# A decoder block on one core: activation sums of the second half step made in the out projection, and products reordered

## The chip, the cores and the metric

The kernel runs on one core of one Trainium2 chip. The metric is the device time of one execution in microseconds. Engines: TensorE (PE), which multiplies; VectorE (DVE) and ScalarE (ACT), which do the elementwise work; GpSimd (POOL); and SyncE (SP), which here issues most transfers. Each engine works through its own list of instructions in a fixed order and waits where an operand isn't ready.

## The reference, cut to what matters

```python
D_MODEL, SEQ, D_FF = 1024, 512, 2816
def rms_norm(x, gain):
    return x * lax.rsqrt(jnp.mean(x * x, axis=-1, keepdims=True) + eps) * gain
def swiglu(h, w_gate, w_up, w_down):
    return (jax.nn.silu(h @ w_gate) * (h @ w_up)) @ w_down

x = x + 0.5 * swiglu(rms_norm(x, ffn1_norm), ffn1_w_gate, ffn1_w_up, ffn1_w_down)
h = rms_norm(x, mix_norm)
g_a, g_b, z_uv, z_q, z_k, z_v = split(h @ w_in)
y_a = gmlp_chunk_mixer(z_uv, ...)                  # 8 groups, chunks of 128 positions
y_b = diff_attention(q, k, v, positions, ...)      # 8 heads, causal
m = sigmoid(g_a) * (y_a @ a_w_proj) + sigmoid(g_b) * (y_b @ b_w_proj)
x = x + m @ w_out
x = x + 0.5 * swiglu(rms_norm(x, ffn2_norm), ffn2_w_gate, ffn2_w_up, ffn2_w_down)
```

## The kernel before, in words

Everything is float32 and lies feature-major: the eight tiles `x_0` to `x_7` have 128 features by 512 positions. A product is made exactly enough by splitting each operand into a rounded part and the rest (`split`: a cast on ACT, line 139, and a subtraction on DVE, line 140) and multiplying hi by hi, hi by lo and lo by hi: three matmuls (`mm3`, lines 125 to 127). So each weight tile of 128 by 1024 costs a transfer, a cast and a subtraction before PE can use it.

The program has three parts. **Half step one** (`ffn` with pool `ff1`) and **half step two** (`ff2`) are the same function: 22 blocks of hidden features, two to a `q`, so 11 steps q = 0 to 10. The mixing stage stands between.

A step q makes gate and up products of two hidden blocks. The first two steps of either half step are plain (`plain_quad`): 4 x 24 matmuls of 512 columns. The others (`quad`) use a seven-product scheme on 2 x 2 blocks: seven products of 24 matmuls with 256 columns each. The factors are sums of weight blocks (`total`, line 311, on DVE: `w_sum`) and sums of activations (`half_sums`: `s_hi`, `s_lo`, four sums for each pair of feature tiles kt and kt + 4, lines 222 to 227, and a split). Products named A take plain activations (`xg_hi`, `xg_lo`), those named S take sums. The sums are made while the plain steps run, called at q = 1. `kept` (line 331) copies a bank out; line 350 adds S0's running result to p7 before S3 adds into the same bank. Lines 346 and 352 form the parts of g, line 357 multiplies by `r_bc`, the norm's factor for each position, line 358 is the Silu. After steps 3, 7 and 10 a group of down projections follows: eight output tiles, 24 matmuls of 512 columns each (18 in the last group), which add up in `y`. Behind the last group `y` is scaled by r (line 396) and the residual, read again into `back`, is added (line 397).

The norm's factor comes from squares on ACT (lines 186 and 189), added on DVE (190), summed over features by two matmuls with ones (195, 196), and `r_bc` on ACT and DVE (`norm_scale`). In half step one the squares are called (`prepare1`) after the first pair's products f = 0 of step 0.

In the mixing stage units of projections are pumped between the steps of attention. `turn_weights` transposes the attention weights of a head and splits them into `at_hi`, `at_lo`. The last units are `add_out`: its `evacuate` adds the out projection to `x1` (line 879), makes `xg_hi` (ACT, line 181) and `xg_lo` (DVE, line 182) for half step two, and adds squares. They run in the order n = 0, 4, 1, 5, 2, 6, 3, 7.

Tiles come from pools with a fixed number of buffers; a scheduler orders each engine's instructions from the program and the pools.

Of the kernel before, what the change touches and what calls it, by code (L numbers as in the profile page):

```python
# [58 lines left out]
def decoder_block(  # L59
# [87 lines left out]
    nc.gpsimd.dma_start(out=gains, in_=cols)  # L147
# [62 lines left out]
    def half_sums(pool, norm):  # L210
# [3 lines left out]
        def add(kt, x1, x2):  # L214
# [5 lines left out]
            f = pool.tile([P, 4, HT], F32, name="sums", tag=("a_hi", "a_lo")[kt % 2] + str(2 + kt // 2))  # L220
# [24 lines left out]
    def ffn(pool, gu, dn, norm, xt, finish, load, prepare, again):  # L245
        a_hi, a_lo = {}, {}
        add_sums, operand = half_sums(pool, norm)
# [25 lines left out]
        def plain_quad(q):  # L273
# [3 lines left out]
            for f in range(2):  # L277
# [86 lines left out]
        y, back = [], []  # L364
        for f0 in range(0, NF, 8):
            n = min(8, NF - f0)
            for q in range(f0 // 2, (f0 + n) // 2):
# [7 lines left out]
            if f0 + n == NF:  # L375
                for i in range(HK):
                    tag = ("w_sum", "g")[i // 2]
                    back.append(pool.tile([P, 2, T], F32, name="x_again", tag=tag, bufs=2))
# [667 lines left out]
```

## Time and profile before

| | |
|---|---|
| median of 3 timed runs | 1159.12 us (1158.76 to 1159.71) |
| the profiled execution | 1159.7 us, of which span 1158.0 |
| granted TensorE clock, mean | 0.997 |
| PE / PEld busy | 1146.5 (99%) / 996.1 (86%) us |
| DVE / ACT busy | 836.4 (72%) / 590.0 (51%) us |
| chain that ended last | PE 95%, ACT 2%, DVE 1%, DMA 1% |

A row of a timeline gives the start, the duration, engine, line, operation, output and inputs with shapes; in brackets stands the idle time before it on its engine and what ended it. Matmuls are pipelined, so their pace is read from start to start. `x4` after a row means four in sequence, with the time of all.

### The profile page before, as it was taken

The page shows a single profiled execution, that of the slowest core. Times are in us where ns is not written, and L with a number is a line of the kernel's source. Part 1 is how long each engine was busy: PE and PEld are TensorE (multiplying, and loading weights), DVE is VectorE, ACT ScalarE, POOL GpSimd, SP SyncE. Part 2 cuts the span into 40 slices and gives each one's busy share as a digit, 9 for nine tenths or more (in the row PEclk, how much of TensorE's full clock was granted, in tenths as well). Part 3 has the DMA queues.
Part 4 walks back from the last instruction along what each step waited for, and adds up shares of the span by engine and source line. Part 5 has one row for each costly group of instructions (what it writes and reads, how often), then busy time and mean ns, then how long its engine had stood idle before and what let it go on. Part 6 is the DMA issues. An engine that isn't in the chain of part 4 may idle for free.

```text
span 1158.0 us, 16621 instructions
## 1 busy us (share of the span) xinstructions
PE 1146.5 (99%) x6554; PEld 996.1 (86%) x6554; DVE 836.4 (72%) x1356; ACT 590.0 (51%) x856; POOL 30.5 (3%) x58
## 2 busy tenths in 40 slices
PE   8999999999999999999999999999999999999998
PEld 6898899989987888888888887888899899988996
DVE  6995389747877667877878986655887369855975
ACT  6563256424544554657587966334545235523440
POOL 0000000000003000000000000000000000000000
PEclk9999999999999999999999999999999999999999
DMA  8134232512434323222212224235424223431241
GB/s 270 58 117 138 73 97 92 163 56 82 143 131 145 122 80 91 74 91 74 74 55 66 63 76 162 91 120 164 153 74 145 73 74 110 132 122 56 83 155 72
DMA packets 46032, 122.08 MB, mean 105 GB/s; under 512 B 4355, under 2 KB 5411, under 8 KB 45955
## 3 DMA queue, kind: packets, MB, share of 16 engines
q1 hardware_dynamic: 43488, 113.26, 30.9%
q0 software_dynamic: 2464, 7.77, 1.9%
q8 instruction: 51, 0.84, 0.3%
q14 instruction: 29, 0.21, 0.1%
HBM read 114.72 MB, written 6.29 MB: 105 GB/s over the span
## 4 chain that ended last, share of the span: by engine, by line
PE 95%; ACT 2%; DVE 1%; DMA 1%; issue 0%; SPq 0%; DVEq 0%; ACTq 0%
PE bank_acc L324 20%; PE bank_att L324 11%; PE bank_acc L127 11%; PE bank_acc L125 11%; PE bank_acc L126 11%; PE bank_att L127 5%; PE bank_att L126 5%; PE bank_att L125 5%; PE bank_acc L536 4%; PE bank_acc L538 4%; PE bank_acc L537 4%; DMA x<-in_x 1%; PE bank_att L666 1%; PE bank_att L667 1%; PE bank_att L694 1%
## 5 line engine op out<-in xcount | busy, mean ns | idle before, releaser
L139 ACT CAST w_hi<-w_raw 128x1024 fp32r<-128x1024 f32 (+2 forms) x192 | 191.8, 1003 | 282.1 <-PE bank_acc L126 92.6
L140 DVE TENSOR_TENSOR w_lo<-w_raw,w_hi 128x1024 fp32r<-128x1024 f32 (+2 forms) x192 | 223.5, 1168 | 75.2 <-ACT w_hi L139 70.3
L139 ACT CAST w_hi<-w_sum 128x1024 fp32r<-128x1024 f32 x72 | 75.4, 1050 | 140.2 <-PE bank_acc L324 63.0
L324 PE MATMUL bank_acc<-s_lo,w_hi 128*128 128x256 f32 x432 | 121.6, 281 | 0.0
L324 PE MATMUL bank_acc<-s_hi,w_hi 128*128 128x256 f32 x432 | 121.5, 281 | 0.0
L324 PE MATMUL bank_acc<-s_hi,w_lo 128*128 128x256 f32 x432 | 121.4, 281 | 0.0
L140 DVE TENSOR_TENSOR w_lo<-w_sum,w_hi 128x1024 fp32r<-128x1024 f32 x72 | 87.7, 1221 | 27.6 <-ACT w_hi L139 27.6
L125 PE MATMUL bank_acc<-xg_hi,w_hi 128*128 128x512 f32 x224 | 89.5, 400 | 3.1 <-ACT w_hi L139 3.0
L127 PE MATMUL bank_acc<-xg_hi,w_lo 128*128 128x512 f32 x224 | 89.7, 400 | 1.2 <-DVE w_lo L140 1.2
L126 PE MATMUL bank_acc<-xg_lo,w_hi 128*128 128x512 f32 x224 | 89.1, 398 | 0.1
L536 PE MATMUL bank_acc<-w_hi,xg_hi 128*128 128x512 f32 x224 | 88.9, 397 | 0.0
L537 PE MATMUL bank_acc<-w_lo,xg_hi 128*128 128x512 f32 x224 | 88.6, 395 | 0.0
L538 PE MATMUL bank_acc<-w_hi,xg_lo 128*128 128x512 f32 x224 | 88.5, 395 | 0.0
L324 PEld LDWEIGHTS bank_acc<-s_hi,w_lo 128*128 128x128 f32 x432 | 81.7, 189 | 0.0
L324 PEld LDWEIGHTS bank_acc<-s_hi,w_hi 128*128 128x128 f32 x432 | 81.7, 189 | 0.0
L324 PEld LDWEIGHTS bank_acc<-s_lo,w_hi 128*128 128x128 f32 x432 | 81.6, 189 | 0.0
L125 PE MATMUL bank_att<-a_hi,w_hi 128*128 128x512 f32 x176 | 69.4, 395 | 0.0
L125 PE MATMUL bank_acc<-a_hi,w_hi 128*128 128x512 f32 x176 | 69.4, 395 | 0.0
L126 PE MATMUL bank_acc<-a_lo,w_hi 128*128 128x512 f32 x176 | 69.4, 394 | 0.0
L126 PE MATMUL bank_att<-a_lo,w_hi 128*128 128x512 f32 x176 | 69.4, 394 | 0.0
L127 PE MATMUL bank_acc<-a_hi,w_lo 128*128 128x512 f32 x176 | 69.4, 394 | 0.0
L127 PE MATMUL bank_att<-a_hi,w_lo 128*128 128x512 f32 x176 | 69.4, 394 | 0.0
(268 smaller groups left out, 2835.2 us busy)
## 6 DMA issues: line engine op xcount, KB each, us to landing
w_raw<-in_gu SPq DMA_DIRECT2D x86, 512.0 KB, 3.7
w_raw<-in_dn SPq DMA_DIRECT2D x32, 512.0 KB, 3.6
w_raw<-in_w_qk SPq DMA_DIRECT2D x16, 512.0 KB, 3.6
w_raw<-in_dn SPq DMA_DIRECT2D x16, 384.0 KB, 3.3
w_raw<-in_w_v SPq DMA_DIRECT2D x8, 512.0 KB, 3.6
w_raw<-in_w_ga SPq DMA_DIRECT2D x8, 512.0 KB, 3.5
w_raw<-in_w_gb SPq DMA_DIRECT2D x8, 512.0 KB, 3.5
w_raw<-in_w_pb SPq DMA_DIRECT2D x8, 512.0 KB, 3.5
```

What stands on the lines that cost most here:

```text
L125: nc.tensor.matmul(ps, lhsT=lhi, rhs=rhi, start=first, stop=False)
L126: nc.tensor.matmul(ps, lhsT=lhi, rhs=rlo, start=False, stop=False)
L127: nc.tensor.matmul(ps, lhsT=llo, rhs=rhi, start=False, stop=last)
L139: latest["hi"] = nc.scalar.copy(hi, src)
L140: latest["lo"] = nc.vector.tensor_tensor(lo, src, hi, op=ALU.subtract)
L324: nc.tensor.matmul(o, lhsT=l[:, s], rhs=r, start=first and f == kt == i == 0, stop=kt == HK - 1 and i == 2, skip_group_check=True,)
L536: nc.tensor.matmul(banks[t], lhsT=xg_hi[k][:, ts], rhs=hi[:, s], start=k == 0, stop=False)
L537: nc.tensor.matmul(banks[t], lhsT=xg_hi[k][:, ts], rhs=lo[:, s], start=False, stop=False)
L538: nc.tensor.matmul(banks[t], lhsT=xg_lo[k][:, ts], rhs=hi[:, s], start=False, stop=k == KD - 1)
L666: nc.tensor.matmul(s[m], lhsT=qd[m][:, qs], rhs=kd[m][:, :w], start=True, stop=False)
L667: nc.tensor.matmul(s[m], lhsT=ql[m][:, qs], rhs=kd[m][:, :w], start=False, stop=True)
L694: nc.tensor.transpose(ps[:, j * P : (j + 1) * P], a[:, j * P : (j + 1) * P], ident)
```

## The change

1. The sums of half step two (`sums2`) are made in `add_out`, for each n of 4 to 7, as the tile pair becomes complete; `s_hi` and `s_lo` lie in a pool `pairs` that lasts through the kernel, and raw weights, the halves of `at_hi` and `at_lo`, and the sums before their split in a pool `wide`.
2. Half step two has no plain steps: `plain` is 2 in half step one and 0 in half step two, so its steps 0 and 1 are quads.
3. In a quad the product A12 comes second instead of sixth, and its part of g right after it.
4. In half step one the squares and `norm_scale` are called after the splits of the second pair's weights (f = 1, k = 0).
5. The residual is read again and added in the middle group of down projections; the last group scales and adds only.
6. `at_hi` and `at_lo` are two tiles of half the size each, so that a transposed tile with over two blocks is split in two pieces. `PIECES` goes from 43 to 27, since several pieces lie in `pairs`.
7. The transfer of `gains` is issued by ACT instead of POOL; WARM goes from 8 to 6.

```diff
-    nc.gpsimd.dma_start(out=gains, in_=cols)
+    nc.scalar.dma_start(out=gains, in_=cols)
...
-            f = pool.tile([P, 4, HT], F32, name="sums", tag=("a_hi", "a_lo")[kt % 2] + str(2 + kt // 2))
+            f = room(kt)
...
-            s_hi.append(pool.tile([P, 4, HT], F32R, name=f"s_hi{kt}"))
-            s_lo.append(pool.tile([P, 4, HT], F32R, name=f"s_lo{kt}"))
+            for s, n in ((s_hi, "hi"), (s_lo, "lo")):
+                s.append(pair(f"s_{n}{kt}").rearrange("p a (b t) -> p (a b) t", t=HT))
...
+                    if q == 0 and f == 1 and k == 0:
+                        prepare[0][0](); prepare[0][1]()
...
-                if q == f == 0:
-                    prepare[0]()
...
-            for i, t in enumerate((b11, b12, b22, b21)):
+            for i, t in ((0, b11), (3, b21), (1, b12), (2, b22)):
...
             product(a, b11, "A11", True)
             p1 = kept(a)
+            product(e, b21, "A12", True)
+            nc.vector.tensor_tensor(
+                g[:, :, :HT], e.rearrange("p (f t) -> p f t", **two), p1.rearrange("p (f t) -> p f t", **two), op=ALU.add
+            )
             t3 = total(b12, b22)
             product(c, t3, "S1", True)
...
             product(a, total(b11, b12), "S0")
             nc.vector.tensor_tensor(p7, a, p7, op=ALU.add)
-            product(e, b21, "A12", True)
...
-                if q < 2:
+                if q < plain:
                     plain_quad(q)
...
-                if q == 1:
+                if q == plain - 1:
                     for kt in range(HK):
                         add_sums(kt, xt[kt], xt[kt + HK])
...
+                elif f0 + n < NF:
+                    nc.vector.tensor_tensor(y[j], y[j], ps, op=ALU.add)
+                    nc.vector.scalar_tensor_tensor(y[j], y[j], -0.5, r_bc, op0=ALU.mult, op1=ALU.mult)
+                    xr = scratch()
+                    again(xr, j)
+                    nc.vector.tensor_tensor(y[j], y[j], xr, op=ALU.add)
                 else:
...
+                    t = scratch()
+                    nc.vector.scalar_tensor_tensor(t, ps, -0.5, r_bc, op0=ALU.mult, op1=ALU.mult)
+                    nc.vector.tensor_tensor(y[j], y[j], t, op=ALU.add)
                     finish(j, y[j])
...
-            split(at_hi[:, : i + 1, qs], at_lo[:, : i + 1, qs], src)
+            src = ps.rearrange("p (j q) -> p j q", q=P)
+            for b in range(i // 2 + 1):
+                n = min(2, i + 1 - 2 * b)
+                split(at_hi[b][:, :n, qs], at_lo[b][:, :n, qs], src[:, 2 * b : 2 * b + n, :])
...
                 add_squares(n, xr)
+                if n >= HK:
+                    sums2[0](n - HK, x1[n - HK], xr)
```

Three places in the engines' lists. First DVE in the head: `w_lo` with 256 columns are the first pair's weights, with 1024 those of the pairs behind it. Before:

```order
15 L182 SCALAR_TENSOR_TENSOR xg_lo_117<-x_7_157,gains,xg_hi_109 128x512
16 L190 TENSOR_TENSOR sq_sum<-sq_sum,scratch 128x512 x6
17 L140 TENSOR_TENSOR w_lo<-w_raw,w_hi 128x1024
18 L190 TENSOR_TENSOR sq_sum<-sq_sum,scratch 128x512
19 L140 TENSOR_TENSOR w_lo<-w_raw,w_hi 128x1024 x2
20 L140 TENSOR_TENSOR sq_lo<-sq_sum,sq_hi 128x512
```

And after:

```order
15 L191 SCALAR_TENSOR_TENSOR xg_lo_121<-x_7_161,gains,xg_hi_113 128x512
16 L149 TENSOR_TENSOR w_lo<-w_raw,w_hi 128x1024 x2
17 L199 TENSOR_TENSOR sq_sum<-sq_sum,scratch 128x512 x6
18 L149 TENSOR_TENSOR w_lo<-w_raw,w_hi 128x1024
19 L199 TENSOR_TENSOR sq_sum<-sq_sum,scratch 128x512
20 L149 TENSOR_TENSOR w_lo<-w_raw,w_hi 128x1024
21 L149 TENSOR_TENSOR sq_lo<-sq_sum,sq_hi 128x512
```

Two of the weight subtractions moved ahead of the six additions of squares, and on ACT likewise two casts ahead of the squares.

Second DVE at the entry of half step two, from the last out projection's evacuation (x_7) on. Before:

```order
1019 L879 TENSOR_TENSOR x_7_7040<-x_7_7040,bank_acc 128x512
1020 L182 SCALAR_TENSOR_TENSOR xg_lo_117<-x_7_7040,gains,xg_hi_109 128x512
1021 L190 TENSOR_TENSOR sq_sum<-sq_sum,scratch 128x512
1022 L140 TENSOR_TENSOR sq_lo<-sq_sum,sq_hi 128x512
1023 L140 TENSOR_TENSOR w_lo<-w_raw,w_hi 128x1024 x4
1024 L159 SCALAR_TENSOR_TENSOR scratch<-r_bc 128x512
```

And after, where `w_sum` are the sums of weight blocks for S1 (row 1064) and S2 (row 1065):

```order
1055 L905 TENSOR_TENSOR x_7_7098<-x_7_7098,bank_acc 128x512
1056 L191 SCALAR_TENSOR_TENSOR xg_lo_121<-x_7_7098,gains,xg_hi_113 128x512
1057 L199 TENSOR_TENSOR sq_sum<-sq_sum,scratch 128x512
1058 L233 SCALAR_TENSOR_TENSOR sums<-x_3_7090,gains,scratch 128x256
1059 L234 SCALAR_TENSOR_TENSOR sums<-x_7_7098,gains,scratch 128x256
1060 L235 SCALAR_TENSOR_TENSOR sums<-x_7_7098,neg_gains,sums 128x256
1061 L236 SCALAR_TENSOR_TENSOR sums<-x_7_7098,neg_gains,sums 128x256
1062 L149 TENSOR_TENSOR s_lo_7732<-sums,s_hi_7731 128x1024
1063 L349 TENSOR_TENSOR g<-bank_att,scratch 128x2x256
1064 L320 TENSOR_TENSOR w_sum<-w_raw 128x1024
1065 L320 TENSOR_TENSOR w_sum<-w_sum,w_raw 128x1024
1066 L149 TENSOR_TENSOR w_lo<-w_sum,w_hi 128x1024 x2
```

The four sums, `s_lo`, the part of g with A12 (L349) and two sums of weights now stand between x_7 and the next `w_lo`.

Third DVE at the end of a quad of half step one, around p7 += S0 (L350 before, L363 after) and the first use of S3 (L360, L369). Before:

```order
86 L350 TENSOR_TENSOR scratch<-bank_acc,scratch 128x512
87 L140 TENSOR_TENSOR w_lo<-w_raw,w_hi 128x1024
88 L352 TENSOR_TENSOR g<-bank_att,scratch 128x2x256
89 L357 TENSOR_TENSOR g<-g,r_bc 128x1024
90 L140 TENSOR_TENSOR w_lo<-w_raw,w_hi 128x1024
91 L360 TENSOR_TENSOR g<-bank_acc,g 128x2x256
```

And after:

```order
107 L359 TENSOR_TENSOR g<-bank_att,scratch 128x2x256
108 L366 TENSOR_TENSOR g<-g,r_bc 128x1024
109 L149 TENSOR_TENSOR w_lo<-w_raw,w_hi 128x1024
110 L363 TENSOR_TENSOR scratch<-bank_acc,scratch 128x512
111 L370 TENSOR_TENSOR g<-scratch,g 128x2x256
112 L149 TENSOR_TENSOR w_lo<-w_sum,w_hi 128x1024
113 L320 TENSOR_TENSOR w_sum<-w_sum,w_raw 128x1024
114 L369 TENSOR_TENSOR g<-bank_acc,g 128x2x256
```

The multiplication by r and the weights' `w_lo` moved ahead of p7 += S0; on PE, A12's 24 matmuls no longer stand between S0 and S3, but the first matmuls of what comes next.

## Rows read from the trace of the kernel before

**Rows 1.** The page: busy time, share of the span and instructions of each engine.

```profile
PE 1146.5 (99%) x6554; PEld 996.1 (86%) x6554; DVE 836.4 (72%) x1356; ACT 590.0 (51%) x856; POOL 30.5 (3%) x58
```

**Rows 2.** Stretches: window and length, busy us (count) by engine, clock, DMA share, GB/s.

```profile
core 0: us, PE busy (x) PEld busy (x) DVE busy (x) ACT busy (x) POOL busy (x), PEclk, DMA share, GB/s
21.60:24.90 3.30, 2.90 (x7) 2.35 (x8) 3.30 (x5) 1.78 (x3) 0.00 (x0) 0.50 0.53 153
...
805.70:850.74 45.04, 45.04 (x195) 36.43 (x194) 33.89 (x46) 22.64 (x28) 0.54 (x1) 1.00 0.37 123
850.74:890.57 39.83, 39.83 (x338) 39.82 (x336) 33.96 (x34) 22.05 (x26) 0.00 (x0) 1.00 0.41 133
...
404.00:700.00 296.00, 295.23 (x1422) 241.16 (x1421) 230.63 (x610) 205.71 (x388) 10.49 (x20) 1.00 0.26 80
...
640.00:660.00 20.00, 19.85 (x103) 16.07 (x102) 17.50 (x40) 19.70 (x37) 0.00 (x0) 1.00 0.08 27
```

**Rows 3.** Timeline of PE in the head: start, us, instruction, idle before and releaser.

```profile
18.15 0.40 PE L127 MATMUL bank_att<-xg_hi,w_lo 128*128 128x512 f32 x1
20.07 0.50 PE L125 MATMUL bank_acc<-xg_hi,w_hi 128*128 128x512 f32 x1 [1.52 <-ACT w_hi L139]
...
22.00 0.80 PE L127 MATMUL bank_acc<-xg_hi,w_lo 128*128 128x512 f32 x1 [1.20 <-DVE w_lo L140]
22.59 0.63 PE L125 MATMUL bank_acc<-xg_hi,w_hi 128*128 128x512 f32 x1
...
25.07 0.39 PE L125 MATMUL bank_acc<-xg_hi,w_hi 128*128 128x512 f32 x1
```

**Rows 4.** Timeline of ACT in the head.

```profile
15.35 3.74 ACT L189 ACTIVATE scratch<-x 128x512 f32<-128x512 f32 x7
```

**Rows 5.** Timeline of DVE in the head.

```profile
16.14 4.66 DVE L190 TENSOR_TENSOR sq_sum<-sq_sum,scratch 128x512 f32<-128x512 f32 x6
20.72 1.22 DVE L140 TENSOR_TENSOR w_lo<-w_raw,w_hi 128x1024 fp32r<-128x1024 f32 x1
```

**Rows 6.** Transfers of the head: SP's queue, DMA issues at 10.1 (us to landing), ACT.

```profile
10.11 0.33 SPq L290 DMA_DIRECT2D w_raw<-in_gu  x1
...
w_raw<-in_gu SPq DMA_DIRECT2D x1, 512.0 KB, 6.2
...
5.19 0.72 ACT L181 ACTIVATE xg_hi<-x,gains 128x512 fp32r<-128x512 f32 x1 [2.88 <-DMA gains<-in_cols]
...
7.39 1.36 ACT L181 ACTIVATE xg_hi<-x,gains 128x512 fp32r<-128x512 f32 x2 [0.88 <-DMA x<-in_x]
```

**Rows 7.** Timelines of DVE and ACT, last out projection and the sums.

```profile
805.90 0.69 DVE L879 TENSOR_TENSOR x<-x,bank_acc 128x512 f32<-128x512 f32 x1 [2.22 <-PE bank_acc L127]
...
808.04 0.68 DVE L190 TENSOR_TENSOR sq_sum<-sq_sum,scratch 128x512 f32<-128x512 f32 x1
...
825.16 0.48 DVE L225 SCALAR_TENSOR_TENSOR sums<-x,gains,scratch 128x256 f32<-128x256 f32 x1
825.56 0.48 DVE L226 SCALAR_TENSOR_TENSOR sums<-x,neg_gains,sums 128x256 f32<-128x256 f32 x1
...
825.03 1.04 ACT L139 CAST s_hi<-sums 128x1024 fp32r<-128x1024 f32 x1
```

**Rows 8.** Timeline of DVE, end of a quad of half step two.

```profile
885.09 0.69 DVE L350 TENSOR_TENSOR scratch<-bank_acc,scratch 128x512 f32<-128x512 f32 x1 [0.68 <-PE bank_acc L324]
...
888.65 1.23 DVE L357 TENSOR_TENSOR g<-g,r_bc 128x1024 f32<-128x1024 f32 x1
889.80 1.22 DVE L140 TENSOR_TENSOR w_lo<-w_raw,w_hi 128x1024 fp32r<-128x1024 f32 x1
```

**Rows 9.** Attention weights, 404 to 700: count, duration ns min/median/max, forms.

```profile
L139 ACT CAST at_hi<-bank_att x32: 248/437/588, 468.7 to 690.4; 128x128 fp32r<-128x128 f32 x8, 128x256 fp32r<-128x256 f32 x8, 128x384 fp32r<-128x384 f32 x8, 128x512 fp32r<-128x512 f32 x8
L140 DVE TENSOR_TENSOR at_lo<-bank_att,at_hi x32: 281/487/692, 469.6 to 691.4; 128x128 fp32r<-128x128 f32 x8, 128x256 fp32r<-128x256 f32 x8, 128x384 fp32r<-128x384 f32 x8, 128x512 fp32r<-128x512 f32 x8
```

**Rows 10.** Timeline of DVE at the end.

```profile
1153.52 0.69 DVE L396 TENSOR_TENSOR y<-y,r_bc 128x512 f32<-128x512 f32 x1
1154.25 0.69 DVE L397 SCALAR_TENSOR_TENSOR y<-y,x_again 128x512 f32<-128x512 f32 x1
```

More of the change, by code (lines that the diff above doesn't have):

```diff
@@ L42 @@
 PI32 = 3.1415925
-PIECES = 43
+PIECES = 27
 RAWS = 2
-WARM = 8
+WARM = 6
 HK = KD // 2
@@ L103, in any_bank, with pair, wide_tile @@
         return bank(acc if turn_of[0] else att)
+    def pair(name, dtype=F32R):
+        return pairs.tile([P, 2, T], dtype, name=name, tag="pair")
+    def wide_tile(name, shape, dtype):
+        return wide.tile(shape, dtype, name=name, tag="wide")
     def scratch():
@@ L204, in norm_scale, with half_sums @@
         rsqrt_newton(r_bc, v, t)
-    def half_sums(pool, norm):
+    def half_sums(norm, room):
         s_hi, s_lo = [], []
@@ L243, in half_sums, with ffn @@
         return add, operand
-    def ffn(pool, gu, dn, norm, xt, finish, load, prepare, again):
+    def ffn(pool, gu, dn, sums, xt, finish, load, prepare, again, plain):
         a_hi, a_lo = {}, {}
-        add_sums, operand = half_sums(pool, norm)
+        add_sums, operand = sums
         turns = {"w": 0, "raw": 0}
@@ L362, in quad @@
             split(*activated(q), g)
-        y, back = [], []
+        y = []
         for f0 in range(0, NF, 8):
@@ L371, in ffn @@
                     quad(q)
-                if q == 1:
+                if q == plain - 1:
                     for kt in range(HK):
                         add_sums(kt, xt[kt], xt[kt + HK])
[L375 to L378, printed above, removed]
-                    again(back[i], i)
             for j in range(KD):
@@ L475, in prepare1 @@
                 add_squares(j, xt[j], latest["hi"])
-            norm_scale()
         def constants1():
@@ L485, in finish1, with again1, room1 @@
             nc.gpsimd.dma_start(out=x1_dram[j], in_=y)
-        def again1(t, i):
-            nc.sync.dma_start(out=t, in_=x[:, 2 * i : 2 * i + 2, :])
-        ffn(ff1, gu1, dn1, 0, xt, finish1, load1, {0: prepare1, 5: constants1}, again1)
+        def again1(t, j):
+            nc.sync.dma_start(out=t, in_=x[:, j, :])
+        def room1(kt):
+            return ff1.tile([P, 4, HT], F32, name="sums", tag=("a_hi", "a_lo")[kt % 2] + str(2 + kt // 2))
+        ffn(ff1, gu1, dn1, half_sums(0, room1), xt, finish1, load1, {0: (prepare1, norm_scale), 5: constants1}, again1, 2)
     x1 = []
@@ L495, in decoder_block @@
         half = mix.enter_context(tc.tile_pool(name="half", bufs=PIECES))
-        big = mix.enter_context(tc.tile_pool(name="big", bufs=1))
-        mask = big.tile([P, T], F32, name="mask")
+        only = mix.enter_context(tc.tile_pool(name="only", bufs=1))
+        mask = only.tile([P, T], F32, name="mask")
         nc.gpsimd.memset(mask, 0.0)
@@ L566, in evacuate @@
             def evacuate(t, ps):
-                take = lent if b else piece
-                hi, lo = take(f"v_hi{b}_{t}"), take(f"v_lo{b}_{t}")
+                if b:
+                    hi, lo = lent(f"v_hi{t}"), lent(f"v_lo{t}")
+                else:
+                    v = pair(f"v{t}")
+                    hi, lo = v[:, 0], v[:, 1]
                 r = r_tok[:, t : t + 1]
@@ L688, in turn_weights @@
             if i == 0:
-                weights[h] = [big.tile([P, NT, T], F32R, name=f"at_{n}", tag=f"at_{n}") for n in ("hi", "lo")]
+                weights[h] = [
+                    [wide_tile(f"at_{n}{b}", [P, 2, T], F32R) for b in range(2)] for n in ("hi", "lo")
+                ]
             at_hi, at_lo = weights[h]
@@ L833, in evacuate @@
             def evacuate(ps):
-                store[n] = piece(f"{name}{n}", F32)
+                if name == "ga" and n < 4:
+                    store[n] = piece(f"{name}{n}", F32)
+                elif n % 2 == 0:
+                    t = pair(f"{name}{n}", F32)
+                    store[n], store[n + 1] = t[:, 0], t[:, 1]
                 nc.vector.tensor_tensor(store[n], ps, r_bc, op=ALU.mult)
@@ L958, in finish2, with again2 @@
             nc.sync.dma_start(out=out[:, j, :], in_=y)
-        def again2(t, i):
-            for e in range(2):
-                nc.sync.dma_start(out=t[:, e], in_=x2_dram[2 * i + e])
-        ffn(ff2, gu2, dn2, 2, x1, finish2, None, {0: norm_scale}, again2)
+        def again2(t, j):
+            nc.sync.dma_start(out=t, in_=x2_dram[j])
+        ffn(ff2, gu2, dn2, sums2, None, finish2, None, {0: norm_scale}, again2, 0)
 def _layouts(i):
```

27 lines of the change are left out of this document (12 added, 15 removed).

## The prediction

> **What bounds the kernel now.** I read the page's engine table first. TensorE (PE) is busy 1146.5 of 1158.0 us, 99%; VectorE (DVE) 72%, ScalarE (ACT) 51% [rows 1]. So time falls only if PE gets fewer columns, or if the few microseconds in which it does not run at its pace go. Second, the busy time by stretch shows what that pace is: two plain steps take 45.04 us, with two matmuls of the norm 194 of 512 columns, so 0.232 us each; two quads take 39.83, and in them the weight loads (PEld) are as busy as PE itself [rows 2]. Third, I looked for places where PE starts late. From the first plain step on there is one: the head. At 18.15 the last matmul of the first pair starts; the next should at 18.38 and does at 20.07 (waiting for `w_hi`), two later comes 22.00 (waiting for `w_lo`), and then six run some 0.42 us apart until 25.07 [rows 3]; the granted clock there is 0.50, that is 1.2 GHz for 2.4 [rows 2]. Ten starts from 18.15 to 25.07 should be 2.32 us and are 6.92: 4.60 lost. The cause is on ACT and DVE: seven squares stand on ACT from 15.35 to 19.09 ahead of the casts of the next weights [rows 4], and six additions of squares on DVE from 16.14 to 20.80 ahead of the first `w_lo` [rows 5]. The mixing stage loses little: PE is busy 295.23 of 296, but ACT runs at 19.70 of 20 in its densest part [rows 2].
>
> All sums below are made against the profiled execution, 1159.7 us; the three timed runs have their median 0.58 lower (1159.12), so I take 0.6 off at the end. A measurement of this kernel can tell about 0.2%, 2.3 us, from no change.
>
> **1. The squares of the first step move behind the weights.** The raw tile that PE wants at 18.38 lands at 10.11 + 6.2 = 16.31 [rows 6]. ACT is free by then (its squares start at 15.35 [rows 4]), so the cast (1.04 for this shape [rows 7]) runs 16.31 to 17.35, the `w_lo` (1.22 [rows 5]) to 18.6, and the first gap closes. The second raw tile, issued right behind, I take as landed 1.2 later (nothing on the page gives it alone; PE wants it only after 24 matmuls more, but what follows on ACT moves with it): cast to 18.6, `w_lo` to 19.9. Then come eight squares of 3.74/7 = 0.53 [rows 4], ACT until 22.9, six additions of 4.66/6 = 0.78 [rows 5], DVE until 24.5. The next pair's first `w_hi` comes at 23.9 but its `w_lo`, behind the additions, at 25.8; PE's order after the change takes 24 matmuls and two more before it, 18.38 + 26 x 0.232 = 24.4. A stall of 1.4 stays where 4.60 were: **-3.2** (-2.0 if the clock falls in it too, -4.6 if there is none). WARM 6 and the earlier `gains` give nothing: the first k waits for `gains` at 5.19, but the second waits for x at 7.39 anyway [rows 6].
>
> **2. Two plain steps of the second half step become quads.** 45.04 - 39.83, less two matmuls of the norm (2 x 0.23), which are in the plain stretch and stay in any case [rows 2]: **-4.75**. It holds as far as a quad keeps its pace of 39.83/336 = 0.1185 us per matmul of 256 columns.
>
> The rows show PEld busy 39.82 of 39.83 in quads and 36.43 of 45.04 in the plain steps [rows 2]. The Trainium skill, "TensorE: Matmul & The Clock Gate", section "LDWEIGHTS (loading the stationary operand)", takes a weight load as its 128 columns over 1.2, some 107 ns; by it a quad of 168 matmuls, bound by its loads, is an estimated 17.9 us, term 2 about -8.7 and the result about 1155.8. The trace disagrees, with 118.5 ns per matmul over 336 of them, and the measurement decides: I give that rule no chance here.
>
> **3. A new wait at the entry of the second half step.** Before, the first plain steps need only `xg`, and the sums are made beside them. After, the first quad's third product (S1) needs `s_lo` of the last pair of feature tiles, whose x7 comes out of the last out projection. Walked with the durations of before: DVE adds x7 at 805.90, and the `sq_sum` behind it ends 808.72; four sums 0.40 apart end 810.43; cast of the sums 1.04, to 811.5; `s_lo` 1.22, to 812.77 [rows 7]. Here the order of DVE decides (the excerpt): behind `s_lo` stands g = A12 + p1 (L349, 0.69), and only behind that the sum of weights for S1 (1.22, to 814.5), its cast on ACT (to 815.6), the sum for S2 on DVE (to 815.8), then `w_lo` (to 816.9) [rows 5, 7, 8]. PE has A11 from 805.70 to 808.54 and A12 to 811.39, and would start S1's third matmul at 811.63; it starts at 816.97. **+5.3**, between 4.2 (if `s_lo` comes earlier, L349 still waits for the end of A12) and 5.6 (if every hand-over costs 0.05 more). In the other 19 quads the weights of S1 stand ahead of L349 in DVE's order, so this happens once. In the out projection the other three sets of sums (4 x 0.40 + 1.22, 2.8 us each two units) lie in DVE's idle time, 2.22 us a unit [rows 7].
>
> The head shows what such a wait costs beyond itself: after PE idled to 20.07 and to 22.00 the granted clock fell from 2.4 to 1.2 GHz [rows 2], and six matmuls took 2.48 instead of 1.39 us [rows 3]; with the one at 22.00 (0.59 to the next instead of 0.23) that is 1.45. PE idles longer here. **+1.45**, between 0 and 2.3.
>
> **4. The order of products in a quad.** Before, S0 is followed by A12's 24 matmuls, 2.84 us, then S3, which adds into the bank that p7 += S0 (L363, L350 before) has to have read. After, A12 is gone from there; in PE's order 9 to 17 matmuls of the next A11 (1.07 to 2.0 us), or five of the down projection (1.16; four, 0.93, before the last groups), stand between. In before's quad p7 += S0 starts at 885.09 with DVE idle ahead of it [rows 8]; after, g x r (1.22) and `w_lo` (1.15 apart) come first. Walked quad by quad through DVE's order, L363 ends 1.05 us after S0 in most, 1.3 to 1.45 where a weight sum more is ahead. Against 0.93 to 1.16 that is 0 to 0.04 in nine quads, 0.3 to 0.45 in some five: **+1.5** (0.3 to 3.5). What hides it is DVE's spare time: 33.9 of 39.8 busy over two quads [rows 2].
>
> **5. The mixing stage.** The attention weights lie in halves, so for i = 2 and 3 of each head there is one more cast and one more subtraction: 16 each. From 248 ns for 128 columns to 588 for 512 a cast is 0.135 fixed, a subtraction (281 to 692) 0.14 [rows 9], 2.2 and 2.3 us in all. But in the changed kernel the second half's cast waits for the first half's subtraction on DVE, about 0.42, and ACT stands: some 0.5 to 0.7 each, 8 to 11 us of ACT spread over 220 us in which ACT has 70% [rows 2]. PE is ahead of ACT in most of it. **+1.0** (-1 to +4; below zero since the order of some other rows there shifts too, by one row in ten).
>
> **6. The tail.** After the last matmul three dependent operations run on DVE, 0.73 apart [rows 10]; the change leaves two: **-0.7**. The residual is read earlier, in the middle down group, where a unit is 24 matmuls (5.56) and DVE has about 1.9 more: nothing.
>
> Sum: -3.2 - 4.75 + 5.3 + 1.45 + 1.5 + 1.0 - 0.7 = +0.6, so 1160.3 in a profiled execution and **1159.7** for the median. What the plain steps give, the wait at their place takes back.
>
> **Rivals.** *Faster: only what is certain.* S3 finds its bank read in time, the split halves stay beside PE's work, and the clock holds through the stall: -3.2 - 4.75 + 5.3 - 0.7 = -3.35, 1155.8. For it: DVE has 15% free in quads, ACT 30% in the mixing stage; against it: the stall is longer than the one that halved the clock in the head.
> *Slower: ACT in the mixing stage.* The second cast of each half waits on DVE while queries, keys and scores of the next step queue behind it on ACT. If half of the 11 us reaches PE, term 5 is 5.5 instead of 1.0: +5.1, 1164.2. It decides the sign from about 2 us more than term 5 on. For it: ACT at 19.70 of 20 [rows 2] where PE already shows 0.15 us idle; against it: that is one part of the stage only.
> *The new wait isn't there*, because the weights of S1 come early enough: without term 3 the sum is -6.15, 1153.0. Only if DVE's order on the chip were another than listed, or the last sums much faster.
>
> **How the numbers follow.** Forecast 0.44, faster rival 0.25, slower rival 0.24, no wait 0.07. Within the forecast's own range, 1157 to 1162, most is within 2.3 us of 1159.12: same 0.36, faster 0.03, slower 0.05. The faster rival gives 0.20 faster, 0.05 same; the slower 0.22 and 0.02; the last 0.07 faster. Together faster 0.30, same 0.43, slower 0.27. The range 1155.0 to 1164.5 holds both rivals' middles and leaves out the last and the slower one's upper end. Signs on both sides hold most of the chance, so the forecast's own range, 1157 to 1162, stands beside it.
>
> **What will show it.** The head: PE without the gap at 18.4, one of about 1.4 near 24.4, no half clock. The entry of the second step: PE idle some 4 us at A12's end and 1.1 before S1's third matmul, released by `w_hi` and `w_lo` of the weight sum, with half clock behind it. Quads: gaps of 0 to 0.45 before the first S3, released by DVE L363. Mixing: PE busy within 1 us of 295.2. Two additions in the tail. I am wrong if the entry's stall is under 4 or over 6, if PE idles over 3 us more in the mixing stage, or if quads of 19.92 grow by more than 0.2 each.

## The result and the profile after

| | before | after |
|---|---|---|
| median of the timed runs | 1158.94 us (1158.12 to 1159.71, 4 runs) | 1167.65 us (1165.87 to 1169.58, 4 runs) |
| ratio | | 1.008 (1.0067 to 1.0092) |
| the profiled execution, its span | 1159.7, 1158.0 us | 1167.16, 1165.5 us |

The change makes the kernel slower by 0.8%, some 9 us. The forecast was no change, 1159.7 in 1155.0 to 1164.5.

The engine table of the changed kernel's page, to set beside [rows 1]:

```profile
PE 1147.3 (98%) x6694; PEld 999.0 (86%) x6694; DVE 866.3 (74%) x1406; ACT 605.1 (52%) x887; POOL 28.6 (2%) x57
```

PE's busy time hardly moved although two plain steps became quads: a PE that runs slowly, or that starts 0.1 us late, counts as busy. DVE has 30 us more, ACT 15. So the stretches have to be compared. The boundaries in both traces are the same instructions: the start, the first matmul of step 4 of half step one, the first of the attention part of the mixing stage, of the out projections, of step 4 of half step two, and the end. The columns are window, length, busy time by engine, clock, DMA share, GB/s. The kernel before:

```profile
0.00:141.14 141.14, 135.62 (x739) 116.62 (x739) 96.06 (x117) 70.00 (x93) 1.88 (x8) 0.99 0.41 128
141.14:404.49 263.35, 263.35 (x1712) 239.03 (x1710) 200.57 (x285) 124.47 (x148) 13.76 (x22) 1.00 0.37 116
404.49:760.90 356.41, 355.64 (x1682) 289.85 (x1680) 269.40 (x662) 232.99 (x425) 10.49 (x20) 1.00 0.27 84
760.90:935.06 174.16, 174.16 (x916) 148.38 (x914) 109.99 (x125) 74.88 (x92) 4.35 (x8) 1.00 0.36 116
935.06:1158.00 222.94, 217.70 (x1513) 202.17 (x1511) 160.38 (x167) 87.70 (x98) 0.00 (x0) 0.99 0.32 104
```

The changed kernel:

```profile
0.00:139.20 139.20, 134.18 (x734) 114.53 (x735) 94.12 (x116) 70.59 (x94) 1.39 (x7) 1.00 0.41 130
139.20:404.93 265.73, 264.83 (x1711) 239.09 (x1710) 206.90 (x294) 122.33 (x147) 12.43 (x22) 1.00 0.36 115
404.93:764.79 359.86, 357.29 (x1681) 289.39 (x1680) 271.12 (x678) 241.72 (x447) 10.48 (x20) 1.00 0.27 83
764.79:941.71 176.92, 171.95 (x1060) 153.61 (x1059) 127.70 (x142) 83.68 (x103) 4.32 (x8) 0.99 0.37 115
941.71:1165.50 223.79, 219.04 (x1513) 202.36 (x1511) 166.50 (x176) 86.83 (x98) 0.00 (x0) 1.00 0.32 103
```

| stretch | after less before | forecast for it |
|---|---|---|
| head, two plain steps, two quads, a down group | -1.94 | -3.05 |
| seven quads, two down groups, first projections | +2.38 | +0.5 |
| attention part of the mixing stage | +3.45 | +1.0 |
| out projections, entry, four steps, a down group | +2.76 | +2.3 |
| seven quads, two down groups, tail | +0.85 | -0.2 |
| sum | +7.50 | +0.6 |

(The forecast's +1.5 for S3 is spread here over the 20 quads. The medians differ by 8.7 us and not 7.5: how much is lost in the head and behind the entry varies from one execution to the next, as is shown below.) Two terms carry the miss: S3 in the quads, and the mixing stage. The others I take in turn.

**The head.** PE in the changed kernel, beside [rows 3]; no other wait of over 0.25 us stands between 17 and 53 us:

```profile
25.53 0.50 PE L136 MATMUL bank_acc<-xg_hi,w_lo 128*128 128x512 f32 x1 [1.12 <-DVE w_lo L149]
```

ACT and DVE that lead to it, beside [rows 4, 5]:

```profile
16.19 1.05 ACT L148 CAST w_hi<-w_raw 128x1024 fp32r<-128x1024 f32 x1 [1.17 <-DMA w_raw<-in_gu]
...
17.27 2.49 DVE L149 TENSOR_TENSOR w_lo<-w_raw,w_hi 128x1024 fp32r<-128x1024 f32 x2 [1.46 <-ACT w_hi L148]
19.67 4.67 DVE L199 TENSOR_TENSOR sq_sum<-sq_sum,scratch 128x512 f32<-128x512 f32 x6
24.26 1.22 DVE L149 TENSOR_TENSOR w_lo<-w_raw,w_hi 128x1024 fp32r<-128x1024 f32 x1
```

The cast follows its transfer, the six additions of squares come behind both `w_lo`, and the third `w_lo` ends at 25.48 instead of the walked 25.8. The double gap and the half clock behind it are gone (granted clock 1.00 from 24.0 to 25.4).

**The entry of half step two.** PE and then DVE:

```profile
815.15 0.27 PE L333 MATMUL bank_att<-xg_hi,w_lo 128*128 128x256 f32 x1
819.54 0.39 PE L333 MATMUL bank_att<-s_hi,w_hi 128*128 128x256 f32 x1 [4.12 <-ACT w_hi L148]
819.77 0.28 PE L333 MATMUL bank_att<-s_lo,w_hi 128*128 128x256 f32 x1
820.81 0.58 PE L333 MATMUL bank_acc<-s_hi,w_hi 128*128 128x256 f32 x1 [0.76 <-ACT w_hi L148]
821.18 0.41 PE L333 MATMUL bank_att<-s_hi,w_lo 128*128 128x256 f32 x1
...
815.45 1.23 DVE L149 TENSOR_TENSOR s_lo<-sums,s_hi 128x1024 fp32r<-128x1024 f32 x1 [1.12 <-ACT s_hi L148]
816.59 0.68 DVE L349 TENSOR_TENSOR g<-bank_att,scratch 128x512 f32<-128x512 f32 x1
817.20 1.22 DVE L320 TENSOR_TENSOR w_sum<-w_raw 128x1024 f32<-128x1024 f32 x1
818.45 1.22 DVE L320 TENSOR_TENSOR w_sum<-w_sum,w_raw 128x1024 f32<-128x1024 f32 x1
819.59 2.42 DVE L149 TENSOR_TENSOR w_lo<-w_sum,w_hi 128x1024 fp32r<-128x1024 f32 x2
```

From 815.15 to 821.18 PE starts four matmuls, where 0.47 us would do: 5.56 lost. Behind it, beside the row of half clock in [rows 2]:

```profile
819.40:822.50 3.10, 2.20 (x10) 2.00 (x11) 3.10 (x4) 1.14 (x2) 0.00 (x0) 0.65 0.13 50
822.50:826.00 3.50, 3.50 (x26) 3.50 (x26) 3.40 (x4) 2.53 (x4) 0.00 (x0) 0.82 0.46 139
```

These clocks are means over a stretch with both levels, 2.4 and 1.2 GHz. From 821.18 some 12 matmuls start 0.213 us apart instead of 0.1185, about 1.1 us in all. Together 6.7, where 5.3 + 1.45 stood. Six profiles have this entry without a plain step: the wait costs 5.54 to 5.56 us in each, the half clock behind it 1.2 to 2.5.

**S3 in the quads.** A typical quad of half step one, PE and DVE:

```profile
283.19 0.28 PE L333 MATMUL bank_acc<-xg_hi,w_lo 128*128 128x256 f32 x1
283.44 0.39 PE L333 MATMUL bank_acc<-s_hi,w_hi 128*128 128x256 f32 x1
283.66 0.28 PE L333 MATMUL bank_acc<-s_lo,w_hi 128*128 128x256 f32 x1
...
279.69 0.69 DVE L359 TENSOR_TENSOR g<-bank_att,scratch 128x512 f32<-128x512 f32 x1 [0.67 <-PE bank_att L333]
280.42 1.22 DVE L366 TENSOR_TENSOR g<-g,r_bc 128x1024 f32<-128x1024 f32 x1
281.56 1.22 DVE L149 TENSOR_TENSOR w_lo<-w_raw,w_hi 128x1024 fp32r<-128x1024 f32 x1
282.70 0.68 DVE L363 TENSOR_TENSOR scratch<-bank_acc,scratch 128x512 f32<-128x512 f32 x1
```

No row says "idle" here, yet the start of S3's first matmul is 0.25 behind the one ahead of it and its second 0.22 behind the first, 0.12 each at pace: 0.24 us. The three DVE operations between the end of A22 and p7 += S0 (279.69 to 282.70) take 3.0 us, and S0 takes 2.84: L363 starts when DVE is through, not when S0 ends. DVE has no idle time ahead of L363 in any of the 20 quads, and S3 starts 0.05 us after L363's end in all of them. In the first quad the wait is much longer:

```profile
71.64 0.28 PE L333 MATMUL bank_acc<-xg_lo,w_hi 128*128 128x256 f32 x1
73.00 0.38 PE L333 MATMUL bank_acc<-s_hi,w_hi 128*128 128x256 f32 x1 [1.09 <-DVE scratch L363]
...
67.12 1.23 DVE L320 TENSOR_TENSOR w_sum<-w_raw 128x1024 f32<-128x1024 f32 x1 [0.37 <-DMA w_raw<-in_gu]
...
72.26 0.69 DVE L363 TENSOR_TENSOR scratch<-bank_acc,scratch 128x512 f32<-128x512 f32 x1
```

DVE waits 0.37 us for a transfer at 67.12 and has one `w_lo` more ahead of L363, which ends 2.51 us after S0 (70.44). Summed over the start-to-start distances at S3, the quads lose 5.8 us: 1.36 here, 0.6, 0.4 and 0.7 at 157.8, 178.9 and 198.8, 0.1 to 0.35 in each of the others.

### The profile page after: what moved, and what is told of

The parts are those of the page before. It is cut to its first block, busy times and chain, and to the rows that moved or that the text cites. A ratio compares the mean times of both kernels' runs of the same rounds, so it can differ in the third digit from the quotient of the medians.

```text
span 1165.5 us, 16986 instructions
## 1 busy us (share of the span) xinstructions
PE 1147.3 (98%) x6694; PEld 999.0 (86%) x6694; DVE 866.3 (74%) x1406; ACT 605.1 (52%) x887; POOL 28.6 (2%) x57
## 4 chain that ended last, share of the span: by engine, by line
PE 83%; DVE 6%; ACT 5%; DMA 3%; issue 2%; SPq 0%; DVEq 0%; ACTq 0%
PE bank_acc L333 19%; PE bank_att L333 11%; PE bank_acc L136 9%; PE bank_acc L135 9%; PE bank_acc L134 9%; PE bank_att L136 4%; PE bank_att L135 4%; PE bank_att L134 4%; PE bank_acc L547 4%; PE bank_acc L549 4%; PE bank_acc L548 4%; DMA w_raw<-in_gu 2%; DVE w_lo L149 2%; DVE w_sum L320 1%; ACT scratch L690 1%
## 5 line engine op out<-in xcount | busy, mean ns | idle before, releaser
L333 PE MATMUL bank_acc<-s_hi,w_hi 128*128 128x256 f32 x480 | 137.4, 286 | 2.8 <-DVE scratch L363 2.0
L333 PE MATMUL bank_acc<-s_lo,w_hi 128*128 128x256 f32 x480 | 135.1, 281 | 0.0
L333 PE MATMUL bank_acc<-s_hi,w_lo 128*128 128x256 f32 x480 | 135.0, 281 | 0.0
L149 DVE TENSOR_TENSOR w_lo<-w_sum,w_hi 128x1024 fp32r<-128x1024 f32 x80 | 97.4, 1221 | 29.9 <-ACT w_hi L148 29.8
L333 PEld LDWEIGHTS bank_acc<-s_hi,w_hi 128*128 128x128 f32 x480 | 90.4, 188 | 7.0 <-DVE scratch L363 5.3
L333 PEld LDWEIGHTS bank_acc<-s_lo,w_hi 128*128 128x128 f32 x480 | 90.4, 188 | 0.0
L333 PEld LDWEIGHTS bank_acc<-s_hi,w_lo 128*128 128x128 f32 x480 | 90.4, 188 | 0.0
L136 PE MATMUL bank_acc<-xg_hi,w_lo 128*128 128x512 f32 x192 | 76.8, 400 | 2.2 <-DVE w_lo L149 2.1
L134 PE MATMUL bank_acc<-xg_hi,w_hi 128*128 128x512 f32 x192 | 76.4, 398 | 1.6 <-ACT w_hi L148 1.1
L135 PE MATMUL bank_acc<-xg_lo,w_hi 128*128 128x512 f32 x192 | 76.2, 397 | 0.1
```

Of the source, the lines that this page charges most:

```text
L134: nc.tensor.matmul(ps, lhsT=lhi, rhs=rhi, start=first, stop=False)
L135: nc.tensor.matmul(ps, lhsT=lhi, rhs=rlo, start=False, stop=False)
L136: nc.tensor.matmul(ps, lhsT=llo, rhs=rhi, start=False, stop=last)
L149: latest["lo"] = nc.vector.tensor_tensor(lo, src, hi, op=ALU.subtract)
L333: nc.tensor.matmul(o, lhsT=l[:, s], rhs=r, start=first and f == kt == i == 0, stop=kt == HK - 1 and i == 2, skip_group_check=True,)
```

## The experiments

Each was timed beside the kernel before on the same chip. Times are medians of the timed runs; ratios are to before.

**A12 sixth again** (but for the first quad of half step two):

```diff
+            early = q == plain == 0
-            product(e, b21, "A12", True)
-            nc.vector.tensor_tensor(g[:, :, :HT], e..., p1..., op=ALU.add)
+            if early: ...                                   # as above
             ...
             nc.vector.tensor_tensor(p7, a, p7, op=ALU.add)
+            if not early: ...                               # A12 here
```

> The changed kernel with A12 sixth again in every quad, but for the first quad of half step two (which has no sums to start with). In the changed kernel's trace PE loses some 5.8 us over pace at the first S3 matmuls of the 20 quads, with DVE L363 as the releaser. Theory A (S3 waits for p7 += S0, because A12 no longer covers it): that loss goes, so 1167.6 - 5.5 = about 1162 us, no gap before S3 but in one quad. Rival (DVE is short of time in the quads, by the weight sums and the sums it now makes elsewhere): the gaps move to other products, and the time stays within 2 us of 1167.6.

Measured: 1161.48 (1159.78 to 1162.46), ratio 1.0029 (1.0018 to 1.004); the changed kernel's was 1.008, so it gains 5.9 us. PE's waits from 26 to 400 us and from 800 us on in that trace (line 337 is the quad's matmul there, L368 p7 += S0):

```profile
PE bank_acc L337 <- DVE scratch L368: 0.2, 1, 0.2
...
PE bank_att L337 <- ACT w_hi L148: 4.1, 1, 4.1
PE bank_acc L337 <- ACT w_hi L148: 0.7, 1, 0.7
```

S3's wait is gone but for 0.2 us in one quad, the entry's remains. So the place of A12 makes the quads' loss, and not a lack of DVE time. The edit moves two things at once, though: A12's matmuls stand between S0 and S3 again, and on DVE p7 += S0 comes ahead of the multiplication by r. In a typical quad of this trace DVE idles 0.66 us until S0 is done, and L368 ends 0.89 us after S0 (275.92 to 276.81). That is less than the 1.07 us of the nine matmuls that stand between S0 and S3 in the changed kernel. So p7 += S0 placed ahead of L366 in DVE's list might do with A12 second; no run tests that. The same kernel once more:

> A second look at the changed kernel with A12 sixth: the entry's wait of 5.5 us and its half clock should be there again, and no wait at S3 over 0.3 us.

1160.98 us in one run, with the entry's wait (4.1 us) as in the first, and none listed at S3.

**One plain step at the entry**:

```diff
-        ffn(ff2, gu2, dn2, sums2, None, finish2, None, {0: norm_scale}, again2, 0)
+        ffn(ff2, gu2, dn2, sums2, None, finish2, None, {0: (lambda: None, norm_scale)}, again2, 1)
```

> The changed kernel with one plain step instead of none at the entry of half step two; the sums stay in the out projection. Theory C (the entry's wait is 5.5 us plus 1.2 of half clock, since nothing of the first quad but A11 and A12 runs without the last sums, and its weight sums stand behind L349): the plain step covers it, minus 6.7 and plus 2.4 for one more plain step: about 1163.3. Rival (DVE is behind after the out projection in any case): the wait moves into the second step, 1167 to 1170.

1163.49 (1160.52 to 1165.18), ratio 1.0043 (1.003 to 1.0055): 4.3 us less than the change. From 760 to 920 us PE waits in its trace only once, for L363 (1.2 us). The wait of the entry was the missing cover, and one plain step covers it.

**The mixing stage: both casts first**:

```diff
-                split(at_hi[b][:, :n, qs], at_lo[b][:, :n, qs], src[:, 2 * b : 2 * b + n, :])
+            for b, n in cuts:
+                nc.scalar.copy(at_hi[b][:, :n, qs], src[:, 2 * b : 2 * b + n, :])
+            for b, n in cuts: ...                           # the subtractions
```

> The changed kernel, but a transposed tile's two casts stand together on ACT ahead of its two subtractions on DVE, so that the second cast doesn't wait for the first subtraction. The mixing stage of the changed kernel loses 3.5 us more than before. Theory B (ACT stands at the second cast and the work behind it comes late): the mixing stage gets 2 to 3 us back, about 1165. Rival (the 16 more casts and subtractions themselves, or the other order of the rows around them): within 1 us of 1167.6.

1165.82 (1163.88 to 1168.12), ratio 1.0068 (1.0048 to 1.0087): 1.4 to 1.8 us less, between the two expectations and not clear of the spread by time alone. By its trace the stage takes 358.03 instead of 359.86. Three things differ in that trace: ACT's idle time ahead of second casts, ended by a subtraction (9.5 us in the change), is gone; ACT loads its function tables twice less (below); and PE doesn't wait for the weights of projection b (1.0 us in the change, below). So the run doesn't show that the second casts were the cause, and the next ones speak against it: in the kernel before with halves alone ACT idles 9.1 us in the same way, and the stage grows by 0.44.

**Halves alone, pools alone, both**, in the kernel before:

```diff
-                weights[h] = [big.tile([P, NT, T], ...) for n in ("hi", "lo")]
+                weights[h] = [[big.tile([P, 2, T], ...) for b in range(2)] for n in ("hi", "lo")]
...
-PIECES = 43
+PIECES = 27
...
-                take = lent if b else piece
+                    v = pair(f"v{t}")                        # and so for r, ya, ga4 to ga7, gb
```

> The kernel before with one part of the change alone: the attention weights lie in halves and are split in two pieces. If the halves make the mixing stage's 3.5 us: 1159 + 3.5 = about 1162.5. If the pools (27 pieces, pairs) and the order they give make it: within 1 us of 1159.

> The kernel before with the mixing stage's pools of the change alone: 27 pieces, and values, gates, factors and gated values in 8 pairs; the attention weights stay whole. The halves alone cost 0.44 us of the mixing stage and nothing in the time, the changed kernel 3.45. If the pools make the rest: 1158.5 + 3 = about 1161.5. If only halves and pools together do: within 1 us of before.

> The kernel before with pools and halves of the change together. If the mixing stage's loss comes of these two and of nothing else in the change: 1158.5 + 3.4 = about 1162. If it needs more (the sums of half step two, which lie in the pairs too and in the wide pool): below 1160.

| kernel | median us | ratio to before | the stage, us |
|---|---|---|---|
| before | 1157.88 to 1158.94 beside these | | 356.41 |
| halves | 1158.05 | 1.0004 (0.9994 to 1.0014) | 356.85 |
| pools | 1159.88 | 1.0021 (1.0012 to 1.0031) | 357.32 |
| both | 1162.09 | 1.0033 (1.0021 to 1.0046) | 358.62 |
| the change | 1167.65 | 1.008 (1.0067 to 1.0092) | 359.86 |

The stages' rows, in the order halves, pools, both:

```profile
402.58:759.43 356.85, 355.83 (x1682) 289.71 (x1680) 270.76 (x678) 234.45 (x441) 10.49 (x20) 1.00 0.27 84
...
402.87:760.19 357.32, 356.27 (x1681) 289.52 (x1680) 269.14 (x662) 238.09 (x429) 10.48 (x20) 1.00 0.27 84
...
403.82:762.44 358.62, 357.00 (x1681) 289.50 (x1680) 271.17 (x678) 242.05 (x447) 10.48 (x20) 1.00 0.26 83
```

Halves cost 0.44 and pools 0.91, but together 2.21; the pools alone fit neither of their two expectations. By time both together cost 3.8 us (2.4 to 5.3), more than the stage; where the rest lies isn't shown. ACT's busy time goes from 232.99 to 234.45, 238.09 and 242.05, and most of that is neither casts nor subtractions. It is ACT_TABLE_LOAD, an instruction of 1.283 us that stands where ACT turns from one kind of function to another: 9 in the stage before and with halves, 13 with pools, 15 with both and in the change. The six more lie between the first product of `ya` (643.24 before, 644.53 in the change) and the first of `y` (716.10, 720.46). The loads there, before:

```profile
L844 ACT ACT_TABLE_LOAD x1 | 1.3, 1283 | 0.0
L676 ACT ACT_TABLE_LOAD x1 | 1.3, 1283 | 0.0
L729 ACT ACT_TABLE_LOAD x1 | 1.3, 1283 | 0.0
```

and in the changed kernel, where the exponentials of attention are L690 (L676 before), the reciprocal roots L750 (L729) and the sigmoids L870 (L844):

```profile
L690 ACT ACT_TABLE_LOAD x4 | 5.1, 1283 | 0.1
L750 ACT ACT_TABLE_LOAD x3 | 3.8, 1283 | 0.1
L870 ACT ACT_TABLE_LOAD x2 | 2.6, 1283 | 0.0
```

ACT is busy 55.05 us of 72.86 there before and 62.78 of 75.93 in the change. With the other pools the scheduler puts these functions into an order in which they alternate more often. Over all profiles the stage takes 356.3 to 356.9 us with 9 loads, 357.3 to 358.0 with 13 and 358.6 or more with 15. That is an argument and not a test: no run takes the loads away alone, and PE's listed waits in the stage grow only from 0.6 to 1.3 us with both. Some 1.2 us of the change's 3.45 are still open here.

**The rest of it: reads of x1 beside the weights of projection b.** In the changed kernel PE waits 1.0 us for a `w_lo` at 714. The transfers from 700 to 706 us, and ACT behind them:

```profile
x<-x_dram POOLq DMA_DIRECT2D x8, 256.0 KB, 5.6
...
w_raw<-in_w_pb SPq DMA_DIRECT2D x1, 512.0 KB, 6.7
...
709.93 1.05 ACT L148 CAST w_hi<-w_raw 128x1024 fp32r<-128x1024 f32 x1 [1.55 <-DMA w_raw<-in_w_pb]
```

In the kernel before, the same weights are issued at 693.89, behind two of these reads (693.28 and 693.80), and land in 3.7 us; in the change they are issued at 703.12, behind five. First the reads moved in the program alone:

```diff
+            pump(1)
             x1.append(residual.tile([P, T], F32, name=f"x1_{n}", tag="x"))
```

> The changed kernel with the eight reads of x1 (256 KB each) issued one to a unit of projection b instead of all together at its start. In the changed kernel they start at 700 to 705 us, just ahead of the first weights of projection b, whose transfer then takes 6.7 instead of 3.7 us; PE loses 1.2 us at 713.8. Theory E (the collision of these transfers makes that loss): no gap there, the transfer under 5 us, about 1166.4. Rival (the weights are late because DVE frees their raw tile late): the gap stays within 0.3 us.

1168.21, ratio 1.0084 (1.0061 to 1.0106). It tests nothing: the reads wait only for the last attention products, so the scheduler issues them at the same time as before. The weights took 7.2 us and PE's wait was there, 1.5. With a true dependence:

```diff
+        pump(2)
+        behind = latest["hi"]
...
+            tc.add_manual_dep(load.ins, behind.ins.name, late, reason="behind the weights")
```

> The changed kernel with the eight reads of x1 made to wait for the split of projection b's second output, some 15 us later. Theory E (their collision with the first weights of projection b makes the 1.2 us gap at 713.8): that transfer takes under 4.5 us, no gap there, about 1.2 to 1.5 less than the changed kernel: 1166.3. Rival (the raw tile comes free too late for any transfer): the gap stays over 0.6 us.

1166.66 (1165.81 to 1167.98), ratio 1.0075 (1.006 to 1.009). The time's gain is within the spread; its trace is plain. The transfer and the stage:

```profile
w_raw<-in_w_pb SPq DMA_DIRECT2D x1, 512.0 KB, 4.3
...
404.71:763.32 358.61, 356.98 (x1682) 289.37 (x1680) 271.25 (x678) 241.93 (x447) 10.52 (x20) 1.00 0.27 83
```

The gap is gone, and the stage is that of pools and halves alone (358.62). So of the 3.45 some 2.2 go with pools and halves and about 1.25 with the collision. Five profiles have this stage as the change has it; it takes 359.21 to 360.66 us in them, with 0.4 to 1.5 of wait at projection b, so the second share is 0.6 to 2.0. Reads and weights both come later than before, the weights by more (9.2 against 6.9 us). With pools and halves alone the weights stand behind five reads too and take 5.7 us, but PE doesn't wait; what the rest of the change adds to that isn't shown.

The Trainium skill, "DMA: Bandwidth & Descriptors", section "Issuing engines are not separate DMA queues", says that transfers issued by different engines run on the same 16 DMA engines and interleave; 6.7 us behind five of the reads against 4.3 with no read ahead, with the reads on POOL's queue and the weights on SP's, agrees.

**Single parts in the kernel before: head, and head with the tail**:

```diff
+                    if q == 0 and f == 1 and k == 0:
+                        prepare[0]()
...
-                if q == f == 0:
-                    prepare[0]()
```

> The kernel before with one part of the change alone: the squares and the norm's factor of half step one behind the weight splits of the second pair. By the forecast's first term, and the changed kernel's trace (1.6 lost from 18 to 25 us where 4.6 were): -3.0, about 1155.8. Rival (the head is bound by its transfers, and the time comes back at the next pair): within 1 us of before.

1155.94 (1155.01 to 1156.64), ratio 0.998 (0.997 to 0.9989): about 2 us, with no gap from 18 to 25 us in its trace. That is the forecast's bound for the head, -2.0, rather than its value, -3.2, because the kernel before doesn't lose 4.6 us there in every execution. Of its 67 timed beside these experiments, 38 had a mean granted clock of 0.999 or 1.0 and a median of 1157.43 us, 29 a lower clock and 1159.12; the profiled execution, 1159.7 at 0.997, is one of the second kind. All ten of the kernel with the head alone are at 0.999 or 1.0. In four profiles with the old order the first quad starts at 54.92 to 56.83 us, the last being that of the kernel before; in twelve with the new order at 52.03 to 53.96. The gap near 24 us is in seven of these twelve.

> The kernel before with two parts of the change, the head and the earlier reading of the residual. The head alone gave -2. One dependent DVE operation less behind the last matmul: -0.7 more, about 1155.3 beside a before of 1158. Rival (the reads in the middle group cost DVE time that PE waits for): no better than the head alone.

1156.26 (1155.97 to 1157.29), ratio 0.9979 (0.9969 to 0.999): the tail can't be told from nothing by time. In the traces the last matmul's start stands 5.15 us ahead of the end (1149.35 to 1154.5), with the head alone 5.59 (1148.71 to 1154.3): 0.44.

**One plain step without sums in the out projection**, on the same base:

> The same with one plain step in half step two, and its sums made during that step as before (not in the out projection). If a plain step of 22 us covers four sets of sums on DVE (11.3 us) beside its own work: -2.4 more, about 1153. If the sums stand behind r_bc and come late: a wait at S1 of the first quad that takes back 2 us or more, 1155 or above.

1163.36 (1162.65 to 1163.79), ratio 1.0043 (1.0028 to 1.0057): 7 us slower than its base, where the sums come late, as the second expectation has it. PE waits in its first quad of half step two:

```profile
831.12 0.38 PE L324 MATMUL bank_att<-s_hi,w_hi 128*128 128x256 f32 x1 [1.38 <-ACT s_hi L139]
832.57 0.38 PE L324 MATMUL bank_att<-s_lo,w_hi 128*128 128x256 f32 x1 [1.07 <-DVE s_lo L140]
```

and twice more for `w_lo` and `s_lo`, 5.0 us in all. So the sums in the out projection are what makes fewer plain steps possible.

**The parts that help, together**: A12 sixth everywhere, one plain step, both casts first.

> The changed kernel with three edits together: A12 sixth again in every quad, one plain step at the entry of half step two, and the two casts of a transposed tile together. Alone they gave -6.2, -4.2 and -1.8 us against the changed kernel's 1167.65. If the three causes are independent (S3's bank, the entry's wait, ACT in the mixing stage): 1167.65 - 12 = about 1155.5, below the kernel before. If they share one cause (DVE short of time): half of that, about 1161.

1154.53 (1154.04 to 1154.83), ratio 0.9962 (0.9949 to 0.9975): faster than both kernels, 13 us better than the change and 3.4 than before. That is near what independent causes were to give (1155.5), and far from a shared lack of DVE time (1161). PE's longest waits in its trace:

```profile
PE bank_acc L134 <- ACT w_hi L148: 1.3, 1, 1.3
PE bank_att L165 <- DVE eps_col L160: 1.1, 1, 1.1
```

Both lie in the first 7 us. Three of 0.2 to 0.3 lie in the mixing stage, and no other is listed. The same with the reads of x1 behind projection b:

> The three edits together (A12 sixth, one plain step, casts together; 1154.5 us) with the reads of x1 behind projection b's second output. With the casts together there was no gap at projection b, so by either theory within 1 us of 1154.5.

1154.68 (1153.46 to 1155.72), ratio 0.9972 (0.9959 to 0.9984): the same, as there was no gap there to close.

## Why the forecast was wrong, by its steps

1. **Head, -3.2: right for the two profiled executions, too large for the median.** Behind the same 194 matmuls the first quad starts at 56.83 us before and at 53.39 after, 3.4 less. Alone and by time it gave about 2, the bound of that term: the profile that I worked from is of an execution that loses more in the head than most.
2. **Plain steps to quads, -4.75: right** as far as it can be told: the stretch with the entry grew by 2.76, and -4.75 + 6.7 for the entry + 0.8 for S3 in its four quads is 2.75. By itself it was not measured.
3. **Entry, +5.3 and +1.45: right**, 5.56 and about 1.1, through the instructions of the walk (PE fits one matmul of S2 in between). One plain step takes it away.
4. **S3, +1.5: the mechanism right, the size wrong; 5.8 measured** (5.9 by undoing it). Two steps failed. The term put nothing for the start behind a wait: S3's second matmul starts 0.21 to 0.23 us behind its first in all 20 quads (0.22 from 283.44 to 283.66) and not 0.12, as in the 18 quads of the kernel before, where S3 doesn't wait. That is 0.1 us each, 2.1 in all. The other 3.7 are late starts of S3, mis-sized in the walk: L363 was to end 1.05 us after S0 in most quads and 1.3 to 1.45 in some five. It ends 0.89 to 1.14 after S0 in thirteen, near enough, but 1.5 to 2.5 in seven, and five of these make 2.9 us of late starts. The bounds ended at 3.5, because most quads were walked with a DVE that had nearly caught up.
5. **Mixing stage, +1.0: mis-sized; 3.45 measured**, inside the bounds of -1 to +4. The halves, which I costed, are worth 0.44: ACT does idle 9.1 us for the subtractions, as forecast (8 to 11), but hardly any of it reaches PE. The pools stood in the term only as rows in another order, at nothing. They cost 0.9 alone and 1.8 on top of the halves, and bring six more table loads with them; how these reach PE is argued and not shown. The collision at projection b, which the term doesn't have, is about 1.25 more. "ACT has 30% free" is an average; from 644.53 to 720.46 us it was busy 62.78 of 75.93.
6. **Tail, -0.7:** 0.4 to 0.5 in the traces, below what the times can tell.

The slower rival named the mixing stage and its price, 1164.2. The stage came with 3.45, short of its 5.5, and not by the second casts that the rival names; S3 made the rest. The two misses have one sign, and I had given each its middle and not their sum's upper end: 3.5 and +4 at once would have been 1159.7 + 2 + 3 = 1164.7, still 3 short.

## What to carry to other kernels

When an order of products is changed, look at what the moved product covered: 2.84 us of matmuls had hidden a bank's read by a slower engine in every quad, and they were needed elsewhere in only one. Give a step that is only needed at an entry to the entry alone. A chain through a busy engine is to be walked from where that engine comes free, not from where its operand is ready; and small waits below the profile's idle rows are found only from start to start. When pools change, count an engine's table loads too, and not only the operations that the change adds: an order that looks alike can hold more of them. And look whether the profile that a forecast starts from is a typical execution: its head was not.

## What the runs showed of the hardware

- The first matmul behind a wait is followed only after 0.21 to 0.23 us instead of 0.12 (256 columns, 20 quads of the changed kernel): about 0.1 us for each wait, even where S3 itself starts on pace (876.26, 0.11 us behind the matmul ahead of it). Only four of the 20 waits are listed as idle time.
- A transfer of 512 KB (the first weights of projection b) took 3.7 and 4.3 us with no read of 256 KB issued ahead of it from another queue, 3.7 to 4.0 behind one or two, 5.4 to 7.2 behind three, and 5.7 to 7.2 behind five.
- An ACT_TABLE_LOAD took 1.283 us, and the same program parts had 9, 13 or 15 of them in the mixing stage by the order that pools and casts gave.
- After PE had started no matmul from 815.15 to 819.54, the granted clock, a mean of the levels 2.4 and 1.2 GHz, was 0.65 from 819.40 to 822.50 and 0.82 from 822.50 to 826.00; about a dozen matmuls ran at 0.213 us, and 26 in the same place in the kernel with A12 sixth.
